# Hybrid encoder block: dilated keys and values moved through DRAM, and the transfers of P^T issued by GpSimd

## The chip, the cores and the metric

The kernel runs on one core of one Trainium2 chip. The metric is the device time of one execution in microseconds, the median of the runs. The core has five engines that work side by side, each through its own list of instructions in order: PE (TensorE, matmuls and transposes; its weight loads are shown apart as PEld), DVE (VectorE), ACT (ScalarE), POOL (GpSimd) and SP (SyncE, which here only issues DMAs). Waits between engines go by semaphores.

## What is computed

Two layers over 512 tokens of width 1024, 16 heads of 64, all in float32. Layer A is dilated window attention in three dilation groups (dilation 1, 4 and 16), merged by their softmax denominators; layer B is neighbourhood attention on an 8 x 64 grid. The change concerns layer A:

```python
def mixer_a(hn, w_in, w_out, q_gain, k_gain, t5_bias):
    proj = hn @ w_in
    n_qkv = N_DIL_GROUPS * 3 * BRANCH_WIDTH
    qkv = proj[..., :n_qkv].reshape(b, s, N_DIL_GROUPS, 3, N_HEADS, HEAD_DIM)
    gate = proj[..., n_qkv:]
    for g, (window, dilation) in enumerate(DILATED_PAIRS):
        q = rms_norm(qkv[:, :, g, 0], q_gain[g])
        k = rms_norm(qkv[:, :, g, 1], k_gain[g])
        v = qkv[:, :, g, 2]
        ...
        o, lse = dilated_group_attention(q, k, v, t5_bias[...], dilation, reach)
    alpha = jax.nn.softmax(jnp.stack(lses), axis=0)
    y = jnp.sum(alpha[..., None] * jnp.stack(outs), axis=0)
    y = y.reshape(b, s, BRANCH_WIDTH).astype(hn.dtype) * jax.nn.silu(gate)
    return y @ w_out
```

Three softmaxes merged by their denominators are one softmax over the scores of all three groups, and the kernel computes it so.

## The kernel before

**Matmuls.** Each float32 product is three matmuls of a faster format: an operand is split into a high half and a low half, and high x high, high x low and low x high are added (`mm3`). Weights come from DRAM in tiles `wraw` of 1024 columns (three buffers, loaded by SP, L178). ACT casts 512 columns to the high half `wh` (L128), and DVE or POOL subtracts to get the low half `wl` (L134): POOL takes two blocks of five, DVE three. `wh` and `wl` have four buffers each.

**Main and side work.** The loop of layer A goes over eight pairs of heads, `hc` 0 to 7. The main work of a pair (`main_a`) is projections: keys and values of groups 1 and 2 together (tile `rawk`, 512 columns), then queries of the three groups and keys of group 0 (`rawq`, 512 columns), then group 0's values (`v0_a`) and the gate (`gate_a`). Side work (attention of the pair before) is put between the main matmuls by hand: a generator yields, and `run` resumes it when a clock of the code's own (`clock`, an estimate in nanoseconds of the matmuls placed so far) has reached a due time. `yield "wait", key, delay` means: not until `key` has been stamped, and `delay` after that. `later_on(delay, job)` runs a job that much later on the same clock. Only PE's list keeps the order as written; the other engines' lists are ordered by a scheduler, save instructions wrapped in `tc.keep_in_program_order`.

**Keys of groups 1 and 2.** The projection leaves tokens on the partitions and features in the columns. The scores need features on the partitions. `head_norm` sums squares (POOL squares, L282 and L284; DVE sums, L285), takes an inverse root and scales the rows on DVE (L307), for the keys 9000 of the clock later. Then `k_a` transposes on PE: for each of the two groups four 128 x 128 transposes into a PSUM bank (`transpose4`, L213), and DVE copies them to `k12`, times a gain (L544). It waits 22500 after the keys are normed (12500 for pair 0, 10000 for pair 7).

**Values of group 0.** They are projected with features on the partitions, scaled on DVE into `vt` (L521), transposed by four PE transposes in `v_a`, and copied by ACT to `v0` (L632), of which there are two, used in turn.

**Queries.** For pairs 0 to 5 (`moved`) a transposition already goes without PE: DVE transposes each 32 x 32 block in place (`turn_q`, L552), and two steps of DMA through DRAM (`qd`, written at L595, read back in four parts at L601, both issued by SP) put the blocks in their places.

**Scores, softmax, P^T.** `attn_a` does the scores of a pair in two halves `u` of 256 tokens each: per half 12 matmuls of group 0 and 32 of groups 1 and 2 (`log`, L209; the trace shows the latter as 64), softmax on DVE and ACT (L809, L820, L831, L672). The probabilities must be transposed for the product with the values. `turner` has DVE transpose blocks into `tr` (L744), writes `tr` to DRAM (`td`, L753) and reads it back into `pq` in four parts (`pt<-td`, L757), all issued by SP. The first half's scores wait 5200 after the next pair's keys are normed, the second half's 16800. A half is sent 7000 + 2000 u after its scores, its four reads follow 8500 after that, 1200 apart. The product with the values (`weigh`, 24 matmuls, 48 in the trace, `o<-pt`) of a pair comes at the start of the next pair's attention. The last pair (7) uses PE transposes throughout.

**Scales.** ACT makes two copies of the row scales for layer A: `rs_half` (half of them, for the gate) and `rs_trj` (whole, in another order, for `vt`).

Of the kernel before, what the change touches and what calls it, by code (L numbers as in the profile page):

```python
# [22 lines left out]
P = 128  # L23
# [19 lines left out]
def tile_hybrid_encoder(  # L43
# [247 lines left out]
    def head_norm(raw, ss, ns, held, delay=0):  # L291


        rs = wk.tile([P, 32], F32, tag="rs", name="rs")
        rsqrt(nc.vector if ns == 8 else nc.gpsimd, rs[:, : 4 * ns], ss[:, : 4 * ns], 4 * ns, 1.0 / DH)

        def scale():
            for i in range(4):
                by = rs[:, i * ns : (i + 1) * ns].unsqueeze(2)
                if len(raw.shape) == 4:  # L300
                    v = raw[:, :, i, :].rearrange("p (h a f) r -> p f h a r", h=2, f=4)
                    by = rs[:, i * ns : (i + 1) * ns].rearrange("p (f h) -> p f h", h=2)
                    by = by.unsqueeze(3).unsqueeze(4).to_broadcast([P, 4, 2, 2, 32])
                else:
# [34 lines left out]
    rs_n = cp.tile([P, 4], F32, name="rs_n")  # L339
    rs_trj = cp.tile([P, S], F32, name="rs_trj")  # L340
    rs_half = cp.tile([P, S], F32, name="rs_half")
# [99 lines left out]

    def part(n):
        return rk[:, 1024 * n : 1024 * n + 1024].rearrange("p (i c) -> p i c", i=4)

    def project_qk(n, ns, key, hc, guard, first=False, **kw):
# [3 lines left out]
        def evac(i, acc):  # L449
            if not box:  # L450
# [7 lines left out]
                elif key == "rawk":  # L458
                    box.append(part(0))
                    st["v12", hc] = part(1 + hc % 3)  # L460
                else:
                    o = 4 * n * (hc % 3)
                    box.append(rk[:, o : o + 4 * n].rearrange("p (i c) -> p i c", i=4))
                box.append(wk.tile([P, 32], F32, tag="ss", name="ss"))
            raw, ss = box
            if key == "rawq" and moved(hc):
                src = acc.rearrange("p (f a r) -> p f a r", f=4, a=4)
                pieces = [(raw[:, :, i, :].rearrange("p (a f) r -> p f a r", a=4), src)]
            elif key == "rawk":
                pieces = [(raw[:, i, :], acc[:, :256]), (st["v12", hc][:, i, :], acc[:, 256:])]  # L470
            else:
                pieces = [(raw[:, i, :], acc[:, :n])]
            for dst, src in pieces:
                if first:
                    nc.scalar.copy(dst, src)
                else:
                    nc.scalar.activation(dst, src, AF.Copy, scale=rs_n[:, i : i + 1])  # L477
            if not first:
                squares(raw[:, :, i, :] if key == "rawq" and moved(hc) else raw[:, i, : ns * 64], ss, i, ns)

# [8 lines left out]
    def normed(raw, ss, ns, key, hc):  # L489
        head_norm(raw, ss, ns, key == "raw", 9000 if key == "rawk" and 0 < hc < NHC - 1 else 0)  # L490
        if key == "rawq" and moved(hc):
            turn_q(raw)
        st[key, hc] = raw
        stamp[key, hc] = clock[0]

    def first_out():

        raw, ss = st.pop("first")
        for i in range(4):
            for t in (raw, st["v12", 0]):  # L500
                nc.scalar.activation(t[:, i, :], t[:, i, :], AF.Copy, scale=rs_n[:, i : i + 1])
            squares(raw[:, i, :], ss, i, 4)
        normed(raw, ss, 4, "rawk", 0)
# [12 lines left out]
    def v0_a(hc):  # L516
# [3 lines left out]
        vt = wk.tile([P, EXT], F32, tag="vt", name="vt", bufs=1)  # L520
        nc.vector.tensor_mul(trj(vt[:, 64:EXT]), to_trj(acc[0]), trj(rs_trj))  # L521
        nc.gpsimd.tensor_copy(vt[:, 0:64], vt[:, EXT - 64 : EXT])
        st["vt", hc] = vt
        stamp["vt", hc] = clock[0]
# [13 lines left out]
    def k_a(hc):  # L538
        yield "wait", ("rawk", hc), 12500 if hc == 0 else 22500 if hc < NHC - 1 else 10000
        k12 = wk.tile([P, 2, 512], F32, tag="k12", name="k12", bufs=1)  # L540
        raw = st.pop(("rawk", hc))
        for g in range(2):
            tp = transpose4(raw, g * P)
            nc.vector.tensor_scalar(k12[:, g, :], tp, gk[:, g + 1 : g + 2], None, op0=ALU.mult)  # L544
            yield
        st["k12", hc] = k12, st.pop(("v12", hc))
        stamp["k12", hc] = 0

    def turn_q(raw):
# [75 lines left out]
    def v_a(hc):  # L625
# [107 lines left out]
    class turner:  # L733
# [11 lines left out]

        def send(self, dst, wait, pace):

# [4 lines left out]
            src = self.t[:, : 4 * run].rearrange("p (b x) -> p b x", b=4)  # L752
            tc.keep_in_program_order(nc.sync.dma_start(d.rearrange("b p x -> p b x"), src))  # L753

            def read(b):
                src = d[b].rearrange("(a k) x -> k a x", a=4)
                tc.keep_in_program_order(nc.sync.dma_start(place[32 * b : 32 * b + 32], src))  # L757
                self.left -= 1
# [4 lines left out]
    def attn_a(hc):  # L763
# [7 lines left out]
        def scores(u):  # L771
# [381 lines left out]
    def side():  # L1153
# [23 lines left out]
        for hc in range(NHC):  # L1177
            if hc < NHC - 1:
                yield from k_a(hc)
                yield from chain(q_a(hc), v_a(hc))  # L1180
                if moved(hc):
                    yield from st.pop(("land", hc))
                yield from attn_a(hc)
                if hc == 1:
# [114 lines left out]
```

## Time and profile before

| | us |
|---|---|
| median of 3 runs | 850.58 (850.46 to 853.66) |
| the profiled execution | 852.44 |
| its span, first to last instruction | 850.60 |
| one pair of layer A (scores of one pair to scores of the next) | 64.1 |
| layer B with its output product, from 579 on | 271.6 |

In the rows of the views, a line starts with its start and duration in microseconds (timelines and chain), or with line, engine, operation, `out<-in` by the program's names and a count (groups); after the bar of a group come busy microseconds, mean nanoseconds of one, and the idle time of the engine just before them with what ended it. In the view by stretches each engine's busy time is given in the order PE, PEld, DVE, ACT, POOL. `SPq` is SP's queue, where issuing a DMA takes the time shown; the data move afterwards. A PE matmul's shown duration overlaps with its neighbours', so PE's pace is read from starts.

### The profile page before, as it was taken

Reading aid. Unit: us, or ns where it says so; the run is one execution under the profiler, and the core shown is the slowest. Engines: PE = TensorE matmul, PEld = TensorE weight load, DVE = VectorE, ACT = ScalarE, POOL = GpSimd, SP = SyncE. Lnnn points to the kernel's source line nnn. Section 1 sums busy time; section 2 is a strip of 40 time slices with the busy share of each in tenths; the row PEclk is TensorE's granted clock in tenths of the full one; section 3 lists DMA queues with packets and bytes.
Section 4 is the critical chain, followed back from the end, with each engine's and each line's share of the span. In section 5 each row is a group of like instructions: output and inputs, shape, how many; then the busy total and the mean of one; then the engine's idle time right before and its main releaser. Section 6 shows DMA issues by size and latency. Waiting matters only on the chain.

```text
span 850.6 us, 15397 instructions
## 1 busy us (share of the span) xinstructions
PE 842.8 (99%) x5546; PEld 702.5 (83%) x5546; DVE 518.5 (61%) x1336; ACT 431.5 (51%) x923; POOL 309.8 (36%) x494
## 2 busy tenths in 40 slices
PE   9999999999999999999999999999999999999998
PEld 7788878788788788788788787789998898889786
DVE  7354684684674674674675745447567656766642
ACT  7433653653653653652653554355366655665531
POOL 2252441542541541542531341121354335542511
PEclk9999999999999999999999999999999999999999
DMA  7346377477478378378375562264245664555333
GB/s 250 110 126 216 97 228 227 137 226 241 128 227 248 102 228 243 102 230 246 99 236 159 147 191 79 60 241 146 82 143 138 174 175 148 168 163 158 99 97 127
DMA packets 65228, 141.23 MB, mean 166 GB/s; under 512 B 5760, under 2 KB 23104, under 8 KB 65152
## 3 DMA queue, kind: packets, MB, share of 16 engines
q1 hardware_dynamic: 65008, 139.99, 54.5%
q8 instruction: 44, 0.72, 0.3%
q10 hardware_dynamic: 144, 0.26, 0.1%
q14 instruction: 32, 0.26, 0.1%
HBM read 109.11 MB, written 31.12 MB: 165 GB/s over the span
## 4 chain that ended last, share of the span: by engine, by line
PE 94%; ACT 3%; DVE 1%; DMA 1%; issue 0%; DVEq 0%; ACTq 0%
PE acc L209 80%; PE log L209 5%; PE o L209 5%; PE tp L213 3%; ACT p L1084 1%; ACT p L672 1%; DMA x_all<-in_xt 0%; ACT p L831 0%; ACT wh L128 0%; DVE hn_l L397 0%; ACT rawk L477 0%; DMA eb<-lb_d 0%; PE pa L209 0%; PE pl L209 0%; DVE p L820 0%
## 5 line engine op out<-in xcount | busy, mean ns | idle before, releaser
L128 ACT CAST wh<-wraw 128x512 fp32r<-128x512 f32 (+1 forms) x275 | 161.4, 588 | 294.7 <-PE acc L209 258.0
L209 PE MATMUL acc<-wh,hn_h 128*128 128x512 f32 (+1 forms) x768 | 293.8, 383 | 1.6 <-ACT rawq L477 0.8
L209 PE MATMUL acc<-wh,hn_l 128*128 128x512 f32 (+1 forms) x768 | 285.6, 373 | 0.0
L209 PE MATMUL acc<-wl,hn_h 128*128 128x512 f32 (+1 forms) x768 | 285.5, 373 | 0.0
L134 POOL TENSOR_TENSOR wl<-wraw,wh 128x512 fp32r<-128x512 f32 (+1 forms) x110 | 136.9, 1244 | 361.0 <-ACT wh L128 341.7
L134 DVE TENSOR_TENSOR wl<-wraw,wh 128x512 fp32r<-128x512 f32 (+1 forms) x166 | 111.1, 670 | 141.5 <-ACT wh L128 137.0
L209 PEld LDWEIGHTS acc<-wh,hn_h 128*128 128x128 f32 x768 | 144.6, 188 | 29.2 <-issue 4.9
L209 PEld LDWEIGHTS acc<-wh,hn_l 128*128 128x128 f32 x768 | 144.5, 188 | 20.8
L209 PEld LDWEIGHTS acc<-wl,hn_h 128*128 128x128 f32 x768 | 145.0, 189 | 18.9
L209 PE MATMUL acc<-y,wh 128*128 128x512 f32 x256 | 81.3, 399 | 0.0
L209 PE MATMUL acc<-hn_h,wh 128*128 128x512 f32 x192 | 77.1, 401 | 0.9 <-ACT rawq L477 0.6
L209 PE MATMUL acc<-hn_h,wl 128*128 128x512 f32 x192 | 74.9, 390 | 0.0
L209 PE MATMUL acc<-hn_l,wh 128*128 128x512 f32 x192 | 74.8, 390 | 0.0
L672 ACT ACTIVATE p<-p,mn 128x512 f32<-128x512 f32 (+3 forms) x128 | 69.3, 586 | 0.0
L831 ACT ACTIVATE p<-p,mn 128x512 f32<-128x512 f32 (+1 forms) x64 | 44.8, 701 | 44.7 <-DVE mn L820 44.5
L285 DVE TENSOR_REDUCE ss<-sq 128x4 f32<-128x256 f32 (+1 forms) x96 | 48.4, 505 | 31.2 <-POOL sq L284 19.7
L744 DVE STREAM_TRANSPOSE tr<-p 128x512 f32<-128x512 f32 (+1 forms) x80 | 53.7, 684 | 9.9 <-ACT p L672 9.5
L284 POOL TENSOR_TENSOR sq<-rawk 128x256 f32<-128x256 f32 x64 | 40.3, 637 | 48.2 <-ACT rawk L477 45.1
L209 PEld LDWEIGHTS acc<-y,wh 128*128 128x128 f32 x256 | 46.3, 188 | 10.2 <-issue 1.1
L209 PE MATMUL acc<-y,wl 128*128 128x512 f32 x128 | 50.0, 391 | 0.0
L209 PEld LDWEIGHTS acc<-hn_h,wh 128*128 128x128 f32 x192 | 36.1, 188 | 10.8 <-ACT rawk L477 2.1
L209 PEld LDWEIGHTS acc<-hn_h,wl 128*128 128x128 f32 x192 | 36.0, 188 | 7.8
(138 smaller groups left out, 1038.7 us busy)
## 6 DMA issues: line engine op xcount, KB each, us to landing
wraw<-in_w SPq DMA_DIRECT2D x95, 512.0 KB
wraw<-in_w SPq DMA_DIRECT2D x38, 384.0 KB
td<-tr SPq DMA_DIRECT2D x14, 1024.0 KB
pt<-td SPq DMA_DIRECT2D x56, 256.0 KB
qd<-rawq SPq DMA_DIRECT2D x6, 1024.0 KB
qt<-qd SPq DMA_DIRECT2D x24, 256.0 KB
td<-tr SPq DMA_DIRECT2D x6, 896.0 KB
pt<-td SPq DMA_DIRECT2D x24, 224.0 KB
```

The costliest lines, as they stand in the source:

```text
L128: nc.scalar.copy(h, raw)
L134: eng.tensor_sub(l, raw, h.bitcast(F32))
L209: nc.tensor.matmul(o, l, r, **kw)
L213: nc.tensor.transpose(o, i, ident)
L284: nc.gpsimd.tensor_mul(sq, v, v)
L285: nc.vector.tensor_reduce(ss[:, i * ns : (i + 1) * ns], sq.rearrange("p (a b) -> p a b", b=64), axis=AX.X, op=ALU.add)
L672: nc.scalar.activation(pr, pr, AF.Copy, scale=mn[:, 3:4])
L744: nc.vector.transpose(dst, src[:, :n].rearrange("p (i b k) -> p i b k", b=4, k=32))
L831: nc.scalar.activation(row, row, AF.Exp, bias=mn[:, 1:2], scale=-1.0, accum_out=mn[:, 2:3])
L1084: nc.scalar.activation(pr[:, o : o + n], pr[:, o : o + n], AF.Exp, bias=mn[:, 0:1], scale=-1.0, accum_out=mn[:, 2:3])
```

## The change

Keys of groups 1 and 2 of pairs 0 to 6 (`moved_k`) are no longer transposed on PE. The projection is stored in another order of columns, DVE transposes 32 x 32 blocks in place, and `move_k` takes them through DRAM (`kd`: one write, four reads of 32 partitions, all issued by POOL) into `k12`, whose layout changes to four runs of 384. Two ACT instructions then apply the gains in place.

Group 0's values of pairs 0 to 5 travel along: DVE transposes the blocks of `vt` into the last 128 of each 384 columns of `rk_a`, they move with the next pair's keys, and POOL copies them to `v0`, times 2, since `vt` is now scaled by `rs_half`. `rs_trj` is gone. Where PE still transposes `vt`, ACT's copy has the factor 2.

P^T of layer A is written and read by DMAs of POOL in place of SP, later: a half is sent 7400 + 6600 u after its scores, its reads follow 18000 (u = 0) or 16000 (u = 1) after that, 900 apart. The first half's scores wait 7200 in place of 5200. The queries of pairs 6 and 7 wait 15000 in place of 13000.

```diff
         if len(v.shape) == 3:
...
+        elif len(v.shape) == 4:
+            nc.gpsimd.tensor_mul(sq.rearrange("p (g a x) -> p a g x", g=2, a=4), v, v)
...
+            if len(raw.shape) == 5:
+                for g in range(2):
+                    tc.keep_in_program_order(nc.vector.transpose(raw[:, :, g, :, :], raw[:, :, g, :, :]))
...
-        nc.scalar.copy(trj(rs_trj), to_trj(pa))
...
+    moved_k = lambda hc: hc < NHC - 1
+    rk_a = rk[:, :1536].rearrange("p (a y) -> p a y", a=4)
...
         if key == "rawq" and moved(hc):
             turn_q(raw)
+        if key == "rawk" and moved_k(hc):
+            move_k(hc, 17500 if hc else 4000)
...
-        nc.vector.tensor_mul(trj(vt[:, 64:EXT]), to_trj(acc[0]), trj(rs_trj))
+        in_trj = lambda t, order: t.rearrange(f"p ({order}) -> p t r j", t=4, j=4)
+        nc.vector.tensor_mul(
+            in_trj(vt[:, 64:EXT], "t r j"), in_trj(acc[0], "j t r"), in_trj(rs_half, "t j r")
+        )
         nc.gpsimd.tensor_copy(vt[:, 0:64], vt[:, EXT - 64 : EXT])
+        if moved(hc):
+            src = vt[:, :S].rearrange("p (i b x) -> p i b x", i=4, b=4)
+            dst = rk_a[:, :, 256:].rearrange("p b (i x) -> p i b x", i=4)
+            tc.keep_in_program_order(nc.vector.transpose(dst, src))
+            stamp["v", hc] = 0
+            return
...
-        yield "wait", ("rawk", hc), 12500 if hc == 0 else 22500 if hc < NHC - 1 else 10000
-        k12 = wk.tile([P, 2, 512], F32, tag="k12", name="k12", bufs=1)
+        yield "wait", ("rawk", hc), 10000
+        k12 = wk.tile([P, 4, 384], F32, tag="k12", name="k12", bufs=1)
...
+    def move_k(hc, delay):
+        n = 384 if hc else 256
+        d = dr.tile([4, P, 384], F32, name="kd", tag="kd", bufs=2)
+        box = []
+        def write():
+            tc.keep_in_program_order(nc.gpsimd.dma_start(d.rearrange("a p y -> p a y")[:, :, :n], rk_a[:, :, :n]))
+            stamp["k12", hc] = 0
+        def read(a):
+            if not box:
+                box.append(wk.tile([P, 4, 384], F32, tag="k12", name="k12", bufs=1))
+            dst = box[0][32 * a : 32 * a + 32, :, :n]
+            src = d[a].rearrange("(b k) y -> k b y", b=4)[:, :, :n]
+            tc.keep_in_program_order(nc.gpsimd.dma_start(dst, src))
+        def landed():
+            kv = box[0]
+            for g in range(2):
+                k = kv[:, :, P * g : P * g + P]
+                tc.keep_in_program_order(nc.scalar.activation(k, k, AF.Copy, scale=gk[:, g + 1 : g + 2]))
+            if hc:
+                src = kv[:, :, 256:].rearrange("p b (i x) -> p b i x", i=4)
+                dst = v0[(hc - 1) % 2].rearrange("p i (b x) -> p b i x", b=4)
+                tc.keep_in_program_order(nc.gpsimd.tensor_scalar(dst, src, 2.0, None, op0=ALU.mult))
+            st["k12", hc] = kv, st.pop(("v12", hc))
+        later_on(delay, write)
+        for n_, a in enumerate((0, 2, 1, 3)):
+            later_on(delay + 18500, partial(read, a))
+        later_on(delay + 32500, landed)
...
-        yield "wait", ("rawq", hc), 18000 if moved(hc) else 13000
+        yield "wait", ("rawq", hc), 18000 if moved(hc) else 15000
...
-        nc.scalar.copy(v0[hc % 2], tp.rearrange("p (i c) -> p i c", i=4))
+        nc.scalar.mul(v0[hc % 2], tp.rearrange("p (i c) -> p i c", i=4), 2.0)
...
-        def send(self, dst, wait, pace):
+        def send(self, dst, wait, pace, by=nc.sync):
...
-                                k12[hs, g, P * j : P * j + P],
+                                sb(k12[hs], P * g + 32 * j, [[384, 4], [1, 32]]),
...
-                    yield "wait", ("rawk", hc + 1), 5200 if u == 0 else 16800
+                    yield "wait", ("rawk", hc + 1), 7200 if u == 0 else 16800
...
-                send = partial(turned.send, pq[:, 2048 * u : 2048 * u + 2048], 8500, 1200)
-                later_on(7000 + 2000 * u, send)
+                send = partial(turned.send, pq[:, 2048 * u : 2048 * u + 2048], 16000 if u else 18000, 900, nc.gpsimd)
+                later_on(7400 + 6600 * u, send)
...
-                yield from k_a(hc)
-                yield from chain(q_a(hc), v_a(hc))
+                yield from q_a(hc)
                 if moved(hc):
                     yield from st.pop(("land", hc))
+                else:
+                    yield from v_a(hc)
                 yield from attn_a(hc)
```

More of the change, by code (lines that the diff above doesn't have):

```diff
@@ L339, in tile_hybrid_encoder @@
     rs_n = cp.tile([P, 4], F32, name="rs_n")
-    rs_trj = cp.tile([P, S], F32, name="rs_trj")
     rs_half = cp.tile([P, S], F32, name="rs_half")
@@ L469, in evac @@
             elif key == "rawk":
-                pieces = [(raw[:, i, :], acc[:, :256]), (st["v12", hc][:, i, :], acc[:, 256:])]
+                keys = raw[:, i, :], acc[:, :256]
+                if moved_k(hc):
+                    keys = raw[:, :, :, i, :], acc[:, :256].rearrange("p (g a x) -> p a g x", g=2, a=4)
+                pieces = [keys, (st["v12", hc][:, i, :], acc[:, 256:])]
             else:
@@ L477, in evac @@
                     nc.scalar.activation(dst, src, AF.Copy, scale=rs_n[:, i : i + 1])
-            if not first:
-                squares(raw[:, :, i, :] if key == "rawq" and moved(hc) else raw[:, i, : ns * 64], ss, i, ns)
+            if first:
+                return
+            if key == "rawk" and moved_k(hc):
+                v = raw[:, :, :, i, :]
+            elif key == "rawq" and moved(hc):
+                v = raw[:, :, i, :]
+            else:
+                v = raw[:, i, : ns * 64]
+            squares(v, ss, i, ns)
         tile_of = lambda hn: lambda k, i: hn[:, k, P * i : P * (i + 1)]
@@ L492, in normed @@
             turn_q(raw)
+        if key == "rawk" and moved_k(hc):
+            move_k(hc, 17500 if hc else 4000)
         st[key, hc] = raw
@@ L499, in first_out @@
         for i in range(4):
-            for t in (raw, st["v12", 0]):
-                nc.scalar.activation(t[:, i, :], t[:, i, :], AF.Copy, scale=rs_n[:, i : i + 1])
-            squares(raw[:, i, :], ss, i, 4)
+            for t in (raw[:, :, :, i, :], st["v12", 0][:, i, :]):
+                nc.scalar.activation(t, t, AF.Copy, scale=rs_n[:, i : i + 1])
+            squares(raw[:, :, :, i, :], ss, i, 4)
         normed(raw, ss, 4, "rawk", 0)
@@ L543, in k_a @@
             tp = transpose4(raw, g * P)
-            nc.vector.tensor_scalar(k12[:, g, :], tp, gk[:, g + 1 : g + 2], None, op0=ALU.mult)
+            dst = k12[:, :, P * g : P * g + P].rearrange("p b (i x) -> p i b x", i=4)
+            src = tp.rearrange("p (i b x) -> p i b x", i=4, b=4)
+            nc.vector.tensor_scalar(dst, src, gk[:, g + 1 : g + 2], None, op0=ALU.mult)
             yield
```

20 lines of the change are left out of this document (14 added, 6 removed).

## The prediction

> **What bounds the kernel now.** I read the page's busy times and its chain of waits first, then the chain in order of time, then one period of layer A.
>
> ```profile
> PE 842.8 (99%) x5546; PEld 702.5 (83%) x5546; DVE 518.5 (61%) x1336; ACT 431.5 (51%) x923; POOL 309.8 (36%) x494
> ...
> PE 94%; ACT 3%; DVE 1%; DMA 1%; issue 0%; DVEq 0%; ACTq 0%
> ```
> ```profile
> 221.50:285.60 64.10, 64.10 (x454) 52.12 (x454) 41.13 (x100) 32.26 (x63) 24.76 (x37) 1.00 0.66 193
> ```
> ```profile
> 242.45 22.47 PE acc L209 x99
> ...
> 280.37 3.62 PE o L209 x48
> ```
>
> The third row is one head pair of layer A in the view by stretches (length; PE, PEld, DVE, ACT and POOL busy; granted clock, DMA share, GB/s): PE is busy in all of its 64.10 us at clock 1.00, so whatever leaves PE's list there leaves the span, unless PE then waits for something. The last two are pieces of the chain in time (start, us): 22.47 / 99 = 0.227 us for one 512-column matmul.
>
> **What leaves PE.** The instruction lists of both kernels have 128 transposes of rawk before and 72 after, 32 of vt before and 8 after: 80 gone, 20 groups of four (two groups for each of pairs 0 to 6, one for vt of pairs 0 to 5). No other PE instruction is added or dropped. Their price on PE, from its timeline:
>
> ```profile
> 239.78 0.40 PE L209 MATMUL acc<-wh,hn_l 128*128 128x512 f32 x1
> 240.02 0.60 PE L213 MATMUL tp<-ident,rawk 128*128 128x128 f32 x4
> 240.37 0.48 PE L209 MATMUL acc<-wh,hn_h 128*128 128x512 f32 x1
> 240.69 0.40 PE L209 MATMUL acc<-wl,hn_h 128*128 128x512 f32 x1
> ...
> 241.85 0.60 PE L213 MATMUL tp<-ident,rawk 128*128 128x128 f32 x4
> ...
> 245.04 0.39 PE L209 MATMUL acc<-hn_h,wh 128*128 128x512 f32 x1
> ```
>
> From 239.78 to 245.04 lie two groups and 19 matmul steps: 5.26 - 19 x 0.227 = 0.95, so 0.474 us for a group. (The busy 0.60 is not the price: it overlaps its neighbours.) 20 x 0.474 = 9.5 us.
>
> **What PE gets in return.** Only the layout of k12 differs: the score matmuls at L209 read it in runs of 32 elements, 384 apart, instead of 128 in a row. The weighing matmuls already read pq in such runs:
>
> ```profile
> L209 PE MATMUL log<-k,qt 64*32 64x128 f32 x128 | 2.4, 274 | 0.0
> ...
> L209 PE MATMUL o<-pt,rawk 128*64 128x128 f32 x32 | 2.0, 276 | 0.0
> ```
>
> The other groups of the same period (221.50 to 285.60) that the parts below use, engine by engine:
>
> ```profile
> L134 POOL TENSOR_TENSOR wl<-wraw,wh 128x512 fp32r<-128x512 f32 x8 | 10.3, 1288 | 23.8 <-ACT wh L128 23.8
> ...
> L699 POOL TENSOR_TENSOR y<-gt,y 128x512 fp32r<-128x512 f32 x1 | 1.6, 1569 | 0.0
> ...
> L522 POOL COPY vt<-vt 128x64 f32<-128x64 f32 x1 | 0.8, 771 | 1.4 <-DVE vt L521 1.4
> ...
> L128 ACT CAST wh<-wraw 128x512 fp32r<-128x512 f32 x20 | 12.4, 620 | 23.3 <-PE acc L209 21.5 <-DVE rs L116 1.8
> ...
> L544 DVE TENSOR_SCALAR k<-tp,gk 128x512 f32<-128x512 f32 x2 | 1.4, 712 | 0.0
> ...
> L552 DVE STREAM_TRANSPOSE rawq<-rawq 128x512 f32<-128x512 f32 x4 | 2.7, 692 | 0.0
> ...
> L521 DVE TENSOR_TENSOR vt<-acc,rs_trj 128x512 f32<-128x512 f32 x1 | 0.7, 681 | 0.0
> ...
> L512 DVE TENSOR_TENSOR gt<-gt,rs_half 128x512 f32<-128x512 f32 x1 | 1.4, 1437 | 0.0
> ```
>
> 276 against 274 ns: 1% of the 2.4 us that the period spends there, under 0.2 us over layer A. I take 0.1.
>
> **DVE and ACT.** Per period DVE loses two k12 copies (2 x 0.71) and gains three transposes of 512 columns (two of rawk, one of vt, 0.69 each): +0.66 on 41.13 busy of 64.10. ACT loses one copy to v0 and gains two scalings of k12 of 512 columns, about a wh cast (0.62) each: +0.6 on 32.26. Both are hidden by PE. Without that cover they would cost 6 x 0.66 = 4 us and 6 x 0.6 = 4 us at most. vt's product reads PSUM with j innermost, which no row shows; I bound it by the 0.68 that it takes now and by gt's 1.44, and take 0.7: only the move of vt waits for it.
>
> **POOL, the part with no row.** POOL issued no DMA before. Now each period puts 15 on it: two td writes, eight pt reads, one kd write, four k12 reads, and one product into v0. SP takes this long for such an issue (its timeline), and the weight halves that share POOL's list stand thus in POOL's:
>
> ```profile
> 243.58 0.94 SPq L757 DMA_DIRECT2D pt<-td  x2
> 244.63 0.38 SPq L753 DMA_DIRECT2D td<-tr  x1
> ```
> ```profile
> 253.87 1.29 POOL L134 TENSOR_TENSOR wl<-wraw,wh 128x512 fp32r<-128x512 f32 x1 [1.64 <-ACT wh L128]
> 259.54 1.29 POOL L134 TENSOR_TENSOR wl<-wraw,wh 128x512 fp32r<-128x512 f32 x1 [4.38 <-ACT wh L128]
> ```
>
> Bounds for one issue c: 0.38 us (SP's td) and 1.57 us (POOL's longest instruction, y). I take 0.77, POOL's own small copy. All 15 at 1.57 would add 23.6 to 24.76 busy, still under 64.10, so it is the order that matters. The worst place in the changed list: between two wl stand seven issues in a row (one pt, four k12, two pt), where the two rows above have 4.38 us free. A late wl hurts PE only after its buffer's slack: wh and wl have four buffers, each block is 12 matmuls, so three blocks (3 x 12 x 0.227 = 8.17 us) lie between a buffer's release and its next use, less 0.62 for the cast and 1.29 for wl: 6.26. So 7c must stay under 4.38 + 6.26 = 10.64, c under 1.52. My 0.77 gives 5.4, no stall; the upper bound 1.57 gives 11.0, 0.35 us late in each of some six periods, 2 us in all. In pairs 1 to 5 the squares come ahead of the seven or after the last pt read. SP loses layer A's 14 writes and 56 reads of P^T, behind which its weight loads stood for some 0.4 us each; as ACT's casts wait for PE and not for data (row of wh), I count no gain.
>
> The Trainium skill, "DMA: Bandwidth & Descriptors", section "Latency and other measured facts", gives about 1 us to the first byte of a DMA issued by GpSimd, for its software emits the descriptors. Were c that 1 us, an estimate from that page, the seven would take 7 us and the sum would be the same.
>
> **Data that comes later.** The code's clock (its own estimate of PE's time) sets when POOL sends and reads. P^T of the second half is the tight one. The rows are ACT's timeline, the page's DMA issues, the chain in time, SP's timeline and the view by stretches:
>
> ```profile
> 404.57 3.03 ACT L477 ACTIVATE rawk<-acc,rs_n 128x256 f32<-128x256 f32 x8
> ```
> ```profile
> wraw<-in_w SPq DMA_DIRECT2D x95, 512.0 KB
> ...
> td<-tr SPq DMA_DIRECT2D x14, 1024.0 KB
> pt<-td SPq DMA_DIRECT2D x56, 256.0 KB
> qd<-rawq SPq DMA_DIRECT2D x6, 1024.0 KB
> qt<-qd SPq DMA_DIRECT2D x24, 256.0 KB
> ```
> ```profile
> 233.20 1.98 PE log L209 x75
> ...
> 462.38 1.59 PE log L209 x44
> ```
> ```profile
> 256.59 0.91 SPq L757 DMA_DIRECT2D pt<-td  x2
> ...
> 264.29 0.43 SPq L595 DMA_DIRECT2D qd<-rawq  x1
> 269.55 0.33 SPq L178 DMA_DIRECT2D wraw<-in_w  x1
> 270.70 1.75 SPq L601 DMA_DIRECT2D qt<-qd  x4
> 274.94 6.18 SPq L178 DMA_DIRECT2D wraw<-in_w  x2
> ```
> ```profile
> 262.00:274.00 12.00, 12.00 (x56) 9.91 (x55) 3.21 (x6) 3.63 (x7) 1.66 (x2) 1.00 0.86 266
> ```
>
> Its scores end at 235.18 (233.20 + 1.98). The last read stood 9000 + 8500 + 3600 = 21100 of the code's clock later, and was issued near 257.0, 21.9 us later: 1.04 us for 1000. Now it stands 14000 + 16000 + 2700 = 32700 later, so near 269.1. On POOL the product into v0, two issues and a wl can stand ahead of it (1.29 + 1.54 + 1.29), so it leaves by about 273. The weighing that needs it was at 280.37 and comes three groups earlier, at 278.95: 6 us for 256 KB. What must pass between 264.29 and then: qd 1024 KB, qt 1024, P^T 1024, one block of weights 512, 3.67 MB; at the 266 GB/s of the last row 13.8 us, done at 278.1. It just fits, and that row's share of 0.86 leaves some rate over. Cost taken: 0. The first half's scores come 2000 later, which gives qt 2 us more. Keys have a whole period, but for pair 6: normed when its copies end (404.57 + 3.03 = 407.6), scaled on ACT 50000 later at 407.6 + 52 = 459.6, ready 1.24 later at 460.8, and its scores start at 462.38: 1.6 us to spare, once. Late by as much, it would cost 1.6; I take 0.
>
> **Sum.** In the profiled execution: span 850.60 - 9.5 + 0.1 = 841.2, and the 1.84 us around the span (its time is 852.44) stay. The median of the runs shown is 850.58, so I forecast 850.58 - 9.4 = 841.2. Alone, this case covers 839.5 to 843.2 (a group between 0.46 and 0.49 us; POOL's 2 us at its bound). A measurement of this kernel can tell 0.5%, 4.3 us, from no change.
>
> **Rivals.**
>
> A, P^T late at the weighing. If both weight blocks of the rows (269.55 and 274.94) share the engines with P^T, 4.19 MB need 15.8 us: 280.0, 1.1 us after PE wants it, in six periods 6.6: 847.8. With half of that, 844.5. For it: the 0.86 in that row, and 1.57 MB more per period (kd written and read). Against: the rate at a full share would be 266 / 0.86 = 309.
>
> B, slower: the stretch of seven issues starves PE of low weight halves. The gain is gone from 7c = 10.64 + 9.4 / 6, c = 1.74, a little above my upper bound. Should each issue wait out one DVE transpose (0.69) on top of 1.57, c is 2.26: 15.8 - 10.64 = 5.2 us late in each of six periods, 31 in all: 872. For it: no row prices an issue on POOL; descriptors of 512 runs for td, 128 for pt, are more than a copy's. Against: DVE is idle 23 us of each period, and POOL 39.
>
> The Trainium skill, "SBUF — State Buffer", section "SBUF: two separate sides", names this mechanism: while DVE runs an operation in a two-port mode, GpSimd cannot write descriptors, and it tells to issue from SP or ACT instead. It counts copies and tensor_scalar between SBUF tiles among these, not transposes; by that B has little to feed on here.
>
> C, the change does not do what it says: PE's freed time is filled at once by weights that come late from DRAM, and the time stays 850.6. Against: PE has no idle time in the period, and ACT's casts wait for PE's buffers (21.5 us in the row of wh), not for data.
>
> **Numbers.** Forecast 0.52; A 0.22 (0.15 near 844.5, 0.07 near 847.8); B 0.20, from 855 up; C 0.06. Faster by over 0.5% (under 846.3): 0.52 + 0.15 + 0.03 of A's upper part = 0.70. Same: 0.04 of A, 0.04 of C and 0.02 of B at c near 1.74, 0.10. Slower: 0.20. For 8 in 10 the range takes the forecast, A and most of C: 839.0 to 854.0, the lower end leaves 2 us for what I count at no gain, above all SP's shorter list.
>
> **What would show it.** Right: tp groups of rawk and vt gone from PE up to pair 6, a period of 62.7 us with PE busy throughout, wl on POOL still waiting for ACT. A shows as PE waiting ahead of L209 o for pt, in every period. B shows as PE idle ahead of acc with POOL's wl as releaser, after the seven issues. Pair 6 would show ACT held at the scaling of k12 and PE held at its scores, once. The forecast falls if one issue on POOL takes 1.6 us or more, or if DMA in the stretch before the weighing stays under 250 GB/s.

## The result, and the profile after

The changed kernel takes 879.88 us (median of 6 runs, 875.24 to 887.51), the kernel before 850.63 (6 runs, 850.46 to 853.85): 1.0336 times as long, interval 1.0287 to 1.0384. The forecast was 841.2 us. The profiled execution after is the fastest of the six, 875.24 us with a span of 873.5, 22.9 over the span of before; its granted clock averages 0.991. The account below is of that execution. The other five are 2.2 to 12.3 us longer at granted clocks of 0.982 to 0.989, and no trace shows where.

First the page after: busy time (share of the span) and number of instructions of each engine, and the P^T transfers that GpSimd now issues (KB each, us from issue to landing).

```profile
PE 844.5 (97%) x5466; PEld 700.1 (80%) x5466; DVE 526.3 (60%) x1342; ACT 434.3 (50%) x930; POOL 371.8 (43%) x605
...
td<-tr POOLq DMA_DIRECT2D x14, 1024.0 KB, 5.9
pt<-td POOLq DMA_DIRECT2D x56, 256.0 KB, 7.8
```

The 80 transposes are gone (5546 - 5466), and yet PE is busy for longer and for a smaller share: it waits, and some of its work runs slowly. A piece of P^T takes 7.8 us from issue to landing. The view by stretches says where. A stretch runs from one weighing's start to the next (from 0 to the first, one middle period, pair 5's to pair 6's, and the two after it); columns as in the prediction. Before:

```profile
0.00:152.06 152.06, 149.82 (x791) 121.26 (x792) 87.79 (x196) 75.16 (x144) 54.85 (x84) 1.00 0.58 183
216.18:280.30 64.12, 64.12 (x453) 52.14 (x453) 41.12 (x101) 32.80 (x63) 24.78 (x37) 1.00 0.66 193
408.54:471.03 62.49, 61.72 (x516) 49.57 (x515) 41.73 (x115) 32.68 (x64) 21.68 (x32) 1.00 0.52 155
471.03:525.10 54.07, 54.06 (x414) 43.67 (x414) 33.22 (x92) 27.28 (x55) 20.60 (x35) 1.00 0.55 157
525.10:548.92 23.82, 23.82 (x222) 19.05 (x221) 12.36 (x36) 11.69 (x25) 4.17 (x6) 1.00 0.19 59
```

And after:

```profile
0.00:155.47 155.47, 145.72 (x767) 117.39 (x768) 88.44 (x194) 75.58 (x144) 66.64 (x102) 1.00 0.62 193
220.60:286.23 65.63, 63.83 (x441) 51.42 (x441) 42.42 (x102) 32.59 (x63) 34.31 (x55) 1.00 0.73 214
418.02:484.77 66.75, 64.30 (x515) 50.76 (x516) 43.22 (x116) 35.73 (x70) 33.18 (x51) 1.00 0.63 183
484.77:546.58 61.81, 54.51 (x406) 43.24 (x405) 33.82 (x93) 27.87 (x57) 23.58 (x42) 0.97 0.43 137
546.58:572.05 25.47, 25.47 (x220) 20.47 (x220) 11.19 (x33) 9.05 (x19) 3.90 (x5) 0.93 0.17 56
```

"Due" below is the time of before less its groups at 0.483 us each (measured further down, in e13), with 2.04 us (nine matmuls of 0.227) moved from the stretch behind pair 6's first weighing to the one ahead of it:

| stretch | before | due | after | lost |
|---|---|---|---|---|
| to the first weighing | 152.06 | 149.2 | 155.47 | 6.3 |
| the four middle periods | 256.48 | 250.7 | 262.55 | 11.9 |
| pair 5's to pair 6's weighing (408.54 / 418.02) | 62.49 | 63.6 | 66.75 | 3.2 |
| to the next weighing | 54.07 | 52.0 | 61.81 | 9.8 |
| to the last weighing | 23.82 | 23.8 | 25.47 | 1.7 |
| the rest, layer B above all | 301.7 | 301.7 | 301.4 | -0.2 |

The losses add up to 32.7: the 22.9 and a gain of 9.7 that was eaten. Two mechanisms show, and the clock adds to both.

**Transfers that come late (the first two rows of the table, and part of the third).** The waits of the changed kernel, in all, times, longest:

```profile
ACT k0h L693 <- DMA qt<-qd: 30.0, 5, 8.2
...
ACT wh L128 <- DMA wraw<-in_w: 7.2, 2, 6.9
...
PE o L209 <- DMA pt<-td: 5.8, 2, 5.1
```

Before, ACT's waits show no wait for qt; the only one of size for a DMA was 6.9 us for wraw. One middle period, engine by engine, shows how the loss comes about. SP issues qd and qt; ACT stands at k0h; PE waits at the weighing, for P^T, and then at the scores (idle time and releaser in brackets; the view names no releaser for the 1.27 us, but the last read of P^T was issued at 277.2, and the last four took 7.7 to 9.3 us to land, 8.6 in the median):

```profile
270.45 0.59 SPq L668 DMA_DIRECT2D qd<-rawq  x1
274.15 0.33 SPq L178 DMA_DIRECT2D wraw<-in_w  x1
279.26 1.75 SPq L674 DMA_DIRECT2D qt<-qd  x4
```
```profile
283.80 0.66 ACT L128 CAST wh<-wraw 128x512 fp32r<-128x512 f32 x1
290.96 1.14 ACT L693 CAST k0h<-qt 128x512 fp32r<-128x512 f32 x1 [6.50 <-DMA qt<-qd]
291.99 0.73 ACT L712 ACTIVATE q0h<-qt,gk 128x512 fp32r<-128x512 f32 x1
292.61 0.61 ACT L128 CAST wh<-wraw 128x512 fp32r<-128x512 f32 x1
```
```profile
286.23 1.97 PE L209 MATMUL o<-pt,rawk 128*64 128x128 f32 x32 [1.27 <-issue]
292.77 0.35 PE L209 MATMUL log<-k0h,q0h 64*128 64x192 f32 x2 [0.58 <-ACT q0h L712]
293.90 0.35 PE L209 MATMUL log<-k0h,q0l 64*128 64x192 f32 x2 [0.30 <-DVE q0l L716]
```

From qd's issue to qt's issue it is 8.8 us (before: 270.70 - 264.29 = 6.4), and some 12 more until ACT has qt. ACT takes its list in order, so it does not cast the next weights while it stands there. The view by stretches has the reason (last two columns: DMA share, GB/s):

```profile
262.00:270.00 8.00, 8.00 (x37) 6.64 (x36) 7.96 (x14) 2.50 (x5) 3.79 (x5) 1.00 1.01 260
270.00:278.00 8.00, 8.00 (x38) 6.60 (x36) 1.56 (x2) 2.99 (x6) 4.94 (x6) 1.00 1.03 334
278.00:286.00 8.00, 6.96 (x31) 5.45 (x29) 2.97 (x6) 4.30 (x11) 4.06 (x7) 1.00 1.04 239
```

The 16 DMA engines are full for 24 us on end and bring (260 + 334 + 239) x 8 = 6.7 MB in them. In the 16 us from 270 on, between qd's issue at 270.45 and the weighing at 286.23, it is (334 + 239) x 8 = 4.6 MB; for the like stretch, 264.29 to 278.95, the prediction had counted 3.67 MB.

**GpSimd's list, in the last two pairs (the rows of 9.8 and 1.7).** GpSimd's timeline as pair 7's keys are normalised, then what PE waits for:

```profile
515.94 0.78 POOL L826 DMA_DIRECT2D td<-tr  x1
516.80 0.19 POOL L108 TENSOR_SCALAR nv<-ss 128x16 f32<-128x16 f32 x1
517.91 1.29 POOL L134 TENSOR_TENSOR wl<-wraw,wh 128x512 fp32r<-128x512 f32 x1 [0.92 <-ACT wh L128]
...
522.96 1.68 POOL L830 DMA_DIRECT2D pt<-td  x3 [0.35 <-DMA td<-tr]
...
525.59 0.22 POOL L120 TENSOR_TENSOR rs<-rs,na 128x16 f32<-128x16 f32 x1
...
541.73 1.29 POOL L134 TENSOR_TENSOR wl<-wraw,wh 128x512 fp32r<-128x512 f32 x1 [7.51 <-ACT wh L128]
542.96 0.59 POOL L830 DMA_DIRECT2D pt<-td  x1
```
```profile
526.33 1.48 PE L213 MATMUL tp<-ident,rawk 128*128 128x128 f32 x4 [3.50 <-DVE rawk L313]
546.58 0.66 PE L209 MATMUL o<-pt,rawk 128*64 128x128 f32 x8 [3.77 <-issue]
```

The reciprocal roots of the keys (L108 to L120), a chain of small instructions, have P^T's issues among them, and the last of P^T's reads stands behind a wl that waits 7.51 us for ACT. PE waits 3.50 us for the keys and 3.77 at the weighing.

**A wait is paid for again.** After such waits the granted clock falls. Stretches of 3 us around the first weighing (PE is idle in the first; the clock is the third column from the right):

```profile
152.00:155.00 3.00, 0.00 (x0) 0.00 (x0) 0.00 (x0) 0.00 (x0) 0.00 (x0) 1.00 1.09 231
155.00:158.00 3.00, 2.53 (x24) 2.56 (x26) 0.00 (x0) 0.00 (x0) 0.00 (x0) 0.54 1.00 301
```

The trace has four such episodes of 3.41 us at half speed in layer A after (none in layer A before), each worth 1.7 us. Two of them stand in the last two pairs: with the waits of 3.50 and 3.77 us they make 10.7 of the 11.5 us lost there.

### The profile page after: what moved, and what is told of

Same layout as the page of the kernel before. It is cut to its first block, busy times and chain, and to the rows that moved or that the text cites. A ratio compares the mean times of both kernels' runs of the same rounds, so it can differ in the third digit from the quotient of the medians.

```text
span 873.5 us, 15338 instructions
## 1 busy us (share of the span) xinstructions
PE 844.5 (97%) x5466; PEld 700.1 (80%) x5466; DVE 526.3 (60%) x1342; ACT 434.3 (50%) x930; POOL 371.8 (43%) x605
## 5 line engine op out<-in xcount | busy, mean ns | idle before, releaser
L134 POOL TENSOR_TENSOR wl<-wraw,wh 128x512 fp32r<-128x512 f32 (+1 forms) x110 | 140.6, 1278 | 298.5 <-ACT wh L128 259.8
L134 DVE TENSOR_TENSOR wl<-wraw,wh 128x512 fp32r<-128x512 f32 (+1 forms) x166 | 113.8, 686 | 142.6 <-ACT wh L128 138.0
L209 PE MATMUL o<-pt,rawk 128*64 128x128 f32 (+1 forms) x448 | 31.9, 297 | 11.1 <-DMA pt<-td 5.8
```

Source lines behind the costliest of these rows:

```text
L134: eng.tensor_sub(l, raw, h.bitcast(F32))
L209: nc.tensor.matmul(o, l, r, **kw)
```

## The experiments

Each ran against the kernel before on the same chip; medians, lowest to highest in brackets. The kernel before, run beside each of them, had medians between 851.0 and 852.9 us.

**The two halves of the change, and who issues.** Four kernels. e1 is the changed kernel with P^T sent by SP at the times of before; e2 is the kernel before with only P^T's issue and times changed; e3 is the changed kernel with SP at the new times; e4 the changed kernel with GpSimd at the old times.

```diff
 e1: -send(..., 16000 if u else 18000, 900, nc.gpsimd); later_on(7400 + 6600 * u, send)
     +send(..., 8500, 1200, nc.sync);                   later_on(7000 + 2000 * u, send)
 e2 (from before): -send(..., 8500, 1200);              later_on(7000 + 2000 * u, send)
     +send(..., 16000 if u else 18000, 900, nc.gpsimd); later_on(7400 + 6600 * u, send)
 e3: -nc.gpsimd  +nc.sync          (times as changed)
 e4: +8500, 1200, nc.gpsimd; later_on(7000 + 2000 * u, send)
```

e1:

> The changed kernel with P^T issued by SP at the old times again (send 7000 + 2000 u after the scores, reads 8500 after that, 1200 apart); keys and values still go through DRAM on POOL. Late-read theory (the reads of P^T now fall on the writing and reading of the queries in the last 20 us before the weighing, and queries and P^T land late): the loss is gone and the 9.5 us of transposes show, 841 to 847. Rival, the extra 1.57 MB per pair of kd fills the DMA engines: still above 855. Rival, ACT's and DVE's extra work: above 850 with no wait for qt.

e2:

> The kernel before with only the P^T part of the change: issued by POOL at the new times; keys and values still transposed on PE, first half of scores at 5200. Late-read theory: queries and P^T land late here too, 865 to 885, with ACT waiting at k0h for qt. Rival, the moved keys cause the loss: 849 to 854.

e3:

> The changed kernel with P^T issued by SP, at the new late times. Late-read theory: the time of the reads decides, not the issuer: 865 to 885. Rival, the second queue of POOL takes the DMA engines' turns from SP's queries: 841 to 852.

e4:

> The changed kernel with P^T issued by POOL, at the old early times. Late-read theory: 841 to 852, perhaps some us above the SP version since POOL then waits for td to land ahead of weight halves. Rival, the second queue takes SP's turns: 865 to 885.

| run | P^T by, times | keys | us |
|---|---|---|---|
| e1 | SP, old | through DRAM | 863.56 (861.02 to 869.72) |
| e2 | GpSimd, new | on PE | 872.29 (870.61 to 874.71) |
| e3 | SP, new | through DRAM | 892.73 (888.64 to 893.98) |
| e4 | GpSimd, old | through DRAM | 870.40 (867.70 to 872.11) |
| changed | GpSimd, new | through DRAM | 879.88 |

The first theory, that late P^T is all of it, had e1 and e4 near 841 to 852 and missed both. P^T's move, later and by GpSimd, costs some 20 us by itself (e2), and the moved keys cost 11 by themselves with the gain already in (e1). Together they cost 29, which the scatter does not tell from the sum. The waits of e2, then of e1:

```profile
ACT k0h L620 <- DMA qt<-qd: 21.6, 4, 5.9
```
```profile
ACT wh L128 <- DMA wraw<-in_w: 65.0, 16, 7.5
...
ACT k0h L693 <- DMA qt<-qd: 25.6, 5, 6.2
```

The traces of the two also say where each loses. "Lost" is reckoned as in the table above (e2 keeps its transposes, so its due is the time of before):

| lost, us | e2, P^T alone | e1, keys alone | changed |
|---|---|---|---|
| to the first weighing | 3.6 | 3.2 | 6.3 |
| the four middle periods | 13.7 | 16.5 | 11.9 |
| pair 5's to pair 6's weighing | 1.4 | 3.1 | 3.2 |
| to the next weighing | 3.3 | 0.0 | 9.8 |
| to the last weighing | 0.0 | 0.0 | 1.7 |

In the middle periods either half of the change alone loses as much as both together (e9 below, with the changed kernel's instructions there, lost 14.7). What grows when both are present is the end, the last two rows.

In e3 the late reads of P^T stand behind SP's own waits (ahead of the weighing at 302.10 the last one leaves at 291.79, after qt, which waits for qd), and PE pays at the weighing; the waits of e3:

```profile
PE o L209 <- DMA pt<-td: 24.4, 4, 9.0
ACT k0h L693 <- DMA qt<-qd: 23.2, 4, 8.3
```

So at the late times issuing on GpSimd is the better of the two, by 13 us, though it is not free (e9); at the old times SP is the better, by 7 (e1 and e4).

**Bytes, the later scores, the queries' time.** e5 adds to the kernel before the keys' and values' transfers and nothing that needs them; e6 alone delays the first half of the scores; e7 and e8 pull the queries forward in the changed kernel and in e1.

```diff
 e5: +later_on(delay, write rk -> kd on nc.gpsimd);  +later_on(delay + 18500, read kd -> scratch) x4
 e6: -yield "wait", ("rawk", hc + 1), 5200 if u == 0 else 16800
     +yield "wait", ("rawk", hc + 1), 7200 if u == 0 else 16800
 e7, e8: -yield "wait", ("rawq", hc), 18000 if moved(hc) ...
         +yield "wait", ("rawq", hc), 10000 if moved(hc) ...
```

e5:

> The kernel before with added transfers alone: per pair 768 KB are written from rawk to DRAM and read again in four pieces into a scratch tensor in DRAM, by GpSimd at the times of the moved keys; nothing reads the scratch and the keys still turn on PE. Full engines (the bytes delay qt and the weights): the version with P^T early lost 863.6 + 9.5 - 850.6 = 22 us to the way of the keys, so 860 to 873, with ACT waiting for qt at k0h or for wraw. Order (the later scores, scalings and waits of the changed list cost it, not the bytes): 850 to 853 and no wait of ACT for DMA.

e6:

> The kernel before with the first half of the scores 2000 later on the code's clock and nothing else. Full engines: the bytes are the same, 850 to 854. Order: the later scores push P^T's write and the weighing; 857 to 870.

e7:

> The changed kernel with the queries' write and reads (qd, qt) 8000 earlier on the code's clock. Full engines: qt is issued some 8 us earlier and is there before ACT needs it for k0h (30 us of ACT's waits go); P^T's reads then meet less at the end: 855 to 870, with o still waiting a little for pt. Order: 878 to 882, as before this edit.

e8:

> The changed kernel with P^T by SyncE at its old times, and the queries' write and reads 8000 earlier. Full engines: ACT's 25.6 us of waits for qt shrink under 5, but the weights still come late behind the keys' reads: 848 to 858. Order: 861 to 866, as without the earlier queries. Under 848 it would beat the kernel before.

e5 took 856.01 (854.97 to 857.15), e6 852.07 (850.65 to 854.29), both against 852.22; e7 877.52 (875.54 to 879.71), e8 863.40 (861.62 to 869.27). e6 is no change: the later scores cost nothing here. e5's bytes cost 3.8, where 9 to 22 were expected if they filled the engines. And the earlier queries bring nothing that is clear of the scatter, though qt comes sooner. e8's waits, to compare with e1's 65.0 for wraw and 25.6 for qt:

```profile
ACT wh L128 <- DMA wraw<-in_w: 74.7, 20, 7.1
...
ACT k0h L693 <- DMA qt<-qd: 4.1, 5, 1.8
```

The wait for qt is gone (4.1) and the wait for weights has grown (74.7). In e7, where ACT's wait for qt fell from 30.0 to 14.7, PE stood 7.6 us for P^T at o (5.8 in the changed kernel), 6.3 of them at the first weighing. With the engines as full as here, pulling one transfer forward made another late; "qt is late" is a symptom.

**GpSimd's list, SP's waits, fewer bytes.** e9 is the changed kernel with P^T of pairs 6 and 7 alone by SP at the same times. e10 is e8 with the queries' reads back at their old place, so that SP doesn't stand for qd; e11 is e10 with the keys' reads earlier; e12 is e10 with group 0's values left on PE (their transposition on DVE and their product on GpSimd go too; those lines are left out below).

```diff
 e9:  -nc.gpsimd  +nc.gpsimd if hc < 6 else nc.sync
 e10: -later_on(5500, partial(read, a))            +later_on(13500, partial(read, a))      # move_q
 e11: -later_on(delay + 18500, partial(read, a))   +later_on(delay + 9500, partial(read, a))  # move_k
 e12: -n = 384 if hc else 256                      +n = 256
      -yield from q_a(hc)                          +yield from chain(q_a(hc), v_a(hc))
```

e9:

> The changed kernel with P^T of pairs 6 and 7 alone issued by SyncE, at the same times. GpSimd's list: in the changed kernel the time from pair 6's weighing to pair 7's last one (61.8 + 25.5) is 11.4 us over the version with P^T by SyncE (52.0 + 23.8), since pair 7's squares and rsqrt stand among P^T's issues and their waits on GpSimd; the 11.4 go: 866 to 871. Transfers (P^T's lateness itself holds the end, whoever issues it): 877 to 882.

e10:

> P^T by SyncE at its old times, the queries written 8000 earlier, and their reads where they were in the changed kernel (13500 after the write, not 5500). SyncE held: with the short lag SyncE stood 37.6 us for qd with weight loads behind it, and ACT 74.7 us for the weights; with the long lag both go: 849 to 855. Full engines: bytes and their time are about the same, weights and qt stay late: 860 to 866.

e11:

> As the run before, and the keys' reads 9500 after their write, not 18500, so that they stand where the engines have more room and clear of the queries. SyncE held: no change against the run before, within 2 us. Full engines: the crowding near the queries eases: 3 to 8 us less than the run before.

e12:

> As the run before the last (queries early with the long lag), but group 0's values stay on TensorE: six groups of transposes come back (6 x 0.36 = 2.1 us) and 512 KB for each pair leave the engines. Full engines: 3 to 8 us less, net 1 to 6 us less. SyncE held: 2 us more.

e9 took 870.19 (867.77 to 873.99), 9.7 less than the changed kernel. Its last two stretches, against 61.81 and 25.47:

```profile
493.93:546.60 52.67, 52.10 (x405) 42.00 (x405) 31.86 (x92) 26.01 (x54) 18.10 (x32) 1.00 0.58 161
546.60:570.44 23.84, 23.83 (x220) 19.24 (x220) 12.09 (x35) 11.07 (x23) 3.90 (x5) 1.00 0.19 59
```

10.8 us less lie there. The code's times are the same, only the issuer differs: the end of layer A pays for P^T's place in GpSimd's list.

e10 took 866.29 (861.98 to 871.41): SP's waits for qd fell from 37.6 us to 20.1, and ACT's for weights rose from 74.7 to 84.6, so SP standing there is not what makes the weights late. e11 took 861.90 (861.05 to 863.65), 4.4 less, though its runs overlap with e10's, and e12 857.05 (854.88 to 860.38), 9.2 less, though e12 has six groups of transposes more on PE. The chain of waits (shares of the span) and ACT's waits of e10:

```profile
PE 61%; DMA 19%; ACT 8%; DVE 8%; POOL 2%; issue 2%; SPq 0%; ACTq 0%; POOLq 0%; DVEq 0%
```
```profile
ACT wh L128 <- DMA wraw<-in_w: 84.6, 22, 6.9
```

And of e12:

```profile
PE 79%; DMA 8%; DVE 6%; ACT 4%; issue 1%; SPq 1%; POOL 0%; ACTq 0%; DVEq 0%
```
```profile
ACT wh L128 <- DMA wraw<-in_w: 53.4, 16, 6.7
```

With 512 KB for each pair less, DMA's share of the chain falls from 19% to 8% (before the change it was 1%) and ACT waits 31 us less for weights. So fewer bytes move the time, as far as e12's lighter lists on DVE and GpSimd, which no run tests alone, have no part in it.

**The gain alone, and how much of it can be kept.** e13 is the kernel before without the 20 groups (it leaves the keys and values unturned, as e16 does), nothing else moved. e16 is e13 with e5's traffic. e14 is e12 with e11's earlier key reads, e15 is e14 with the queries at the changed kernel's times; e17 and e18 are these two with pair 0's key reads late again.

```diff
 e13: -tp = transpose4(raw, g * P)   +tp = raw[:, :, g * P : g * P + P]     # pairs 0 to 6; v likewise from vt
 e14: -later_on(delay + 18500, ...)  +later_on(delay + 9500, ...)
 e17, e18: +later_on(delay + (9500 if hc else 18500), ...)
```

e13:

> The kernel before without its 20 groups of transposes of the keys (pairs 0 to 6) and of group 0's values (pairs 0 to 5), which are copied unturned; no transfer is added, so this is the gain alone. By the 0.474 us of the prediction 9.5 us less: 841 to 842. By the step from start to start of TensorE's instructions (0.355 for a group) 7.1 us less: 843 to 845. TensorE does not have the gain at all (something else takes its place): 849 to 853.

e14:

> The run without the values' travel (857.0), and the keys' reads 9500 after their write. Full engines: the earlier reads gave 4.4 us with the values and now fewer bytes are read, so 2 to 4 us less: 853 to 855. If the keys' reads do not matter any more: 856 to 858. Under 850 it would beat the kernel before.

e15:

> As the run before with the queries' write and reads at the times of the changed kernel (8000 later, reads 5500 after). Full engines: qt meets less than in the changed kernel, and the weights have the earlier stretch for themselves: 850 to 858. The queries' time matters more than the keys' bytes: 860 to 866.

e16:

> The kernel without the 20 groups, with the added traffic of keys and values as in the run that added it to the kernel before (3.8 us there); nothing waits for what it brings. Bytes alone: the gain less some 4 to 8, since TensorE is now quicker and the transfers are not: 847 to 853. The rest of what P^T early and keys through DRAM lose (863.6) is then the wait for the keys themselves. If it comes near 863, the traffic alone explains that version.

e17:

> The run without the values' travel and with the keys' reads 9500 after their write (857.5), where pair 0's reads alone stand again 18500 after it. There TensorE stood still 5.2 us near 69 for ACT's gt and its clock then fell, and the stretch up to the first weighing took 157.9 us against 150.3 with the late reads, while pairs 2 to 5 had the full gain. Full engines (pair 0's early reads meet the weights): those 6 to 7 us go, 849 to 852, beside the kernel before's 850.6 to 852. If the stretch's loss has another cause (it differs from run to run): 855 to 858.

e18:

> The same with the queries at the times of the changed kernel. Full engines: the first stretch falls from 156.0 to some 150.3 us and 848 to 852 is left, level with the kernel before or 1 to 3 us under it. Another cause: 855 to 858.

| run | us | before, run beside it |
|---|---|---|
| e13 | 845.40 (842.78 to 847.99) | 852.20 |
| e16 | 850.92 (848.35 to 856.30) | 852.20 |
| e14 | 857.54 (857.30 to 859.91) | 852.20 |
| e15 | 857.44 (855.43 to 865.27) | 852.20 |
| e17 | 852.35 (850.46 to 854.90) | 851.00 |
| e18 | 858.20 (852.48 to 861.43) | 851.00 |

e13's periods settle the price of a group:

```profile
215.16:277.83 62.67, 62.67 (x443) 50.96 (x442) 39.81 (x101) 32.16 (x62) 24.05 (x37) 1.00 0.67 200
0.00:152.46 152.46, 147.14 (x768) 118.55 (x768) 86.69 (x196) 74.78 (x143) 55.24 (x84) 0.99 0.58 181
```

64.12 - 62.67 = 1.45 for three groups, 0.483 each. My doubt in e13's expectation (0.355) was wrong, though the whole came nearer to it: the first stretch gave its gain back, with one wait of PE of 1.87 us at 115.92 (for ACT's rawq) and 3.41 us of half clock behind it. With the traffic that nothing waits for (e16) 5.5 us of the gain are lost; e1, where the scores do need what it brings, lies 12.6 us above e16. (In e16, as in e5, the reads land in a scratch tensor in DRAM, not in the keys' buffer.)

e14 had its middle periods right (63.4, 63.6, 63.4 and 63.4 us, with one group of transposes still in each) but lost 5.8 us at the start (157.9 to the first weighing, before 152.1); e17 gave 5.2 of it back (152.7). GpSimd's, ACT's and PE's rows of e14:

```profile
57.91 2.21 POOL L604 DMA_DIRECT2D k<-kd  x4 [0.24 <-DMA kd<-rawk]
```
```profile
71.16 1.14 ACT L128 CAST wh<-wraw 128x512 fp32r<-128x512 f32 x2 [10.62 <-DMA wraw<-in_w]
```
```profile
72.84 0.79 PE L209 MATMUL acc<-wh,hn_h 128*128 128x512 f32 x1 [4.82 <-ACT gt L539]
```

and ACT's of e17, where the same four reads leave GpSimd at 70.01:

```profile
68.10 1.14 ACT L128 CAST wh<-wraw 128x512 fp32r<-128x512 f32 x2 [7.08 <-DMA wraw<-in_w]
```

With four key reads ahead of the weights ACT stands 3.5 us longer at the cast, and the gate's copy out of PE's accumulator (gt), behind it in ACT's list, holds PE for 4.82 us (1.27 in e17), with 6.8 us of half clock after that (none there in e17). With the reads 12 us later the whole is 5.2 us shorter (857.54 to 852.35). The same edit between e15 and e18 brought nothing in the median (857.44 and 858.20, with runs from 852.48 to 865.27), so it does not help everywhere. e17 stands at 1.0014 of before, interval 1.0004 to 1.0024: the best of these kernels gets back to the kernel before and not past it. e18, which differs from it only in the queries' times, was expected level and is 0.7% above.

## Why the prediction was wrong

**The step that failed is "Data that comes later", where the cost was taken as 0.** It counted 3.67 MB between 264.29 and 278.95 as if nothing else were in flight, and read a share of 0.86 as room to spare. In the like stretch after, 270 to 286, 4.6 MB passed, and the engines had been full since 262: the keys' and values' reads (four of 192 KB, issued from 260.7 on), which the count leaves out, and reads of P^T's first half were still under way. The rate was not at fault: some 287 GB/s on average there against the 266 taken, and under the prediction's sign of 250 only in the last 8 us. P^T's last reads took 8.6 us where the step left 6, and PE waited 1.27 us at that period's weighing; what came far too late was qt, and behind it in ACT's order the weights' casts. e2 shows the step by itself: with P^T moved and nothing else, 13.7 us go in the four middle periods and 19.7 in all. The step asked whether P^T arrives before PE needs it; it should have asked, for every transfer of the stretch, what it pushes back. Rival A had this mechanism with P^T as its victim and 1.1 us a period as its price; the four middle periods lost 3.0 each.

**Moved keys were costed as bytes only.** The prediction let 1.57 MB more per period count for rival A and put no price on it. With P^T where it was they lose 16.5 us in the middle periods (e1), while their bytes alone, with nothing waiting for them, cost 3.8 to 5.5 in all (e5, e16).

**GpSimd's issues, a second term put at 0.** The price of one was within its bounds: 0.56 us for a P^T read and 0.80 for its write, against 0.77 taken and 1.6 as the point where the forecast falls. The seven issues in a row (260.19 to 264.2 in that period, 4.0 us where 5.4 were taken) starve nothing: POOL's wl still waits for ACT (259.8 us on the page). But GpSimd's order does cost, at a place that was not looked at: pair 7's normalisation and the last reads of P^T. There 10.8 us come back in e9, against 2 us that the prediction allowed at most. Rival B named the right queue, for the wrong reason and place; that its 872 lies near the time measured is luck.

**What held.** A group of transposes is worth 0.483 us (0.474 taken). The scores with keys in runs of 32 have the same median as before, 269 ns. DVE's and ACT's added work, 8 and 3 us in all, was taken as hidden by PE; no run tests that alone. No gain from SP's shorter list shows. The first half of the scores 2000 later costs nothing (e6), but gave qt no room either.

**Pair 6.** Its period lost 3.2. PE waits 1.58 us there for ACT's copy of rawq out of the accumulator, which softmax work on ACT stands around; e1, e8 and e9, too, take 66 to 67 us for it, where 63.6 are due. e2, with P^T alone, takes 63.9 where 62.5 are due, so most of it comes with the moved keys. The sign that the prediction gave, PE held at pair 6's scores for the scaling of k12, does not show: the scaling ends at 473.5, and the scores start at 474.74 without a wait. Which of ACT's added rows does it was not tried.

What stays open: the 12.6 us between e1 and e16. Both carry the same bytes; e1 also waits for them, reads into the keys' own buffer, scales them on ACT and turns values on DVE. Of the 14.8 us between the spans of their traces 6.8 are clock (e1 has 17.1 us at half speed, e16 3.4) and 5.6 more idle time of PE in layer A (14.2 against 8.6). e12 and e17 show that the size and the time of the transfers move much of what such a kernel loses, but no run says which of e1's additions brings on the waits.

## What to carry to other kernels

A transfer moved in time also costs what it makes late, not only its own delay: before moving work to DMA, take the DMA share of the stretch in which the data must pass, and count what is already in flight as well as what is added. An engine that waits in order (ACT at qt here) turns one late transfer into late work for all that stands behind it. And when an issue is given to a compute engine, read that engine's list at the edges of the loop, where the work between the issues is another, and not only in the middle.

## What was unexpected of the hardware

- The clock can fall after short waits. In e13 1.87 us of idle PE were followed by 3.41 us at half speed, so the wait cost 3.6. Not every such wait is: 1.99 us in the same trace (up to 67.84) were followed by none, nor were 0.77 us in the kernel before, and the wait of 1.58 us in pair 6 was followed by half speed in e17 and not in e14. The Trainium skill, "TensorE: Matmul & The Clock Gate", section "Part 1: The HAM clock gate (the "warmup" mystery)", gives an idle window of about 3.4 us as what brings the half rate. The length of the slow episodes agrees with it (3.41, sometimes 6.83, once 10.24 in e3); the idle time ahead of one was shorter here.
- Full DMA engines moved very different rates here: at a share of 1.01 to 1.04 the three rows above have 239, 260 and 334 GB/s. The Trainium skill, "DMA: Bandwidth & Descriptors", section "Issuing engines are not separate DMA queues", says that transfers issued by SyncE and GpSimd run on the same 16 engines and interleave; the runs agree (qt, issued by SP, is late behind GpSimd's P^T and keys).
- Some kernels with crowded engines scatter more: 12.3 us from lowest to highest in the changed kernel, 9.4 in e10, 3.4 in the kernel before; but 2.2 in e5 and 2.6 in e11. e9, whose instructions are the changed kernel's up to pair 6, took 161.7 us to the first weighing where the changed kernel took 155.5.
